# c spread from a row by TensorE, and the squares of x summed by TensorE ahead of the root's table

## The chip, the cores and the metric

The kernel runs on one core of one Trainium2 chip. The metric is device time in microseconds (us) of one execution; lower is better. Before the change three runs gave 1126.79 (median), 1125.45 and 1129.61 us.

## What is computed

A decoder trunk of two layers over 512 tokens of width 1024, in float32. Each layer is conditioned on a vector `c`: six vectors of width 1024 come from `silu(c) @ ada_w + ada_b`, and they scale, shift and gate the two halves of the layer. What the change touches is the very first step, the conditioned norm ahead of layer 0's projection:

```
def rms_norm(x, g):
    y = xf * lax.rsqrt(jnp.mean(xf * xf, axis=-1, keepdims=True) + EPS)
    return (y * g)
def adaln_params(c, w, b):
    m = jax.nn.silu(c) @ w + b
...
sh1, sc1, g1, sh2, sc2, g2 = adaln_params(c, ada_w[layer], ada_b[layer])
h = rms_norm(x, norm_mix_g[layer]) * (1.0 + sc1) + sh1
xr, gr, q, k, v = jnp.split(h @ ev_w_in[e], 5, axis=-1)
```

Then layer 0 runs a gated recurrence on `xr` (convolution, two gates by block matmuls, a scan), multiplied by `gelu(gr)`, beside a stick-breaking attention on `q`, `k`, `v`.

## The kernel before

x lies transposed in SBUF, channels on the 128 partitions in KC = 8 chunks of 128, tokens (512) along the free dimension. All large products are three matmuls of 512 columns (`mm3`): weights and activations are split into a rounded part and a rest (`whi`, `wlo`, and `hh`, `hl`), where ScalarE (ACT) writes the rounded part and VectorE (DVE) the rest. Weights come by DMA on SyncE's queue (SP) into `raw` tiles, three buffers in rotation; the gate pieces (`graw`, 128 KB) use the same three buffers.

The conditioning products are made on DVE: `ada_col` multiplies a 128x1024 block of `ada_w` with `c_s`, which holds silu(c) on every partition, and sums along the row. `c_s` is loaded by one DMA that repeats the row of c on 128 partitions (L119) and put through silu on ACT (L378).

The head of the kernel runs in this order. ACT: silu of `c_s`, then the table of Sqrt is called up by a dummy activation (`preload`, L326), then four squares of x (L394), two chunks each. DVE adds the two halves of each square (L395) and, in groups 1 and 2, the sum so far (L397); the sums of groups 2 and 3 go through TensorE (PE) against a column of `ones` (which holds 1/1024) into `ms` (L401, 4 calls of one column each). ACT takes the root (`sd`, L405), DVE the reciprocal (L408), PE spreads it over the partitions (`rb`, L412), DVE makes `ht` (L305), ACT `h` (L309), and the first projection product starts (L437). PE fills the time before with `busy(n)`: n products of `ones` with `ones` into a bank `warm` that nothing reads (L387). A call with float32 operands shows as two records in the trace.

These instructions are held in written order by `pin`. The first projection has eight accumulating banks (`qk`), fed chunk by chunk: for each m two conditioning columns, `ht`, the weight's rest and `hl` on DVE. Everything after it is put in order by a scheduler at build time, from its own estimates: an instruction's place on its engine is fixed before the run, and the engine then takes its instructions one after the other, waiting at each until its inputs are there. In layer 0's recurrence the pair of channel blocks (2, 3) follows the pair (0, 1); `pr` and `pi` are a block's gate products, `xcs` their input, `gw` the split gate piece, `gr` the products of the gelu branch. Three DMAs each of `k` and `kl` within SBUF, issued by POOL (L492), run beside it.

Of the kernel before, what the change touches and what calls it, by code (L numbers as in the profile page):

```python
# [9 lines left out]
F32 = mybir.dt.float32  # L10
F32R = mybir.dt.float32r
BF16 = mybir.dt.bfloat16
AF = mybir.ActivationFunctionType
ALU = mybir.AluOpType

P = 128
S = 512
D = 1024
KC = D // P
NB = S // P  # L20
# [47 lines left out]
def trunk(ctx, tc, xT, cvec, cols, adaw, wu, ws, w6, gate, cst, cstb, outT):  # L68
    nc = tc.nc
    V, A, PE = nc.vector, nc.scalar, nc.tensor  # L70

    const = ctx.enter_context(tc.tile_pool(name="const", bufs=1))
# [5 lines left out]
    def mm_bank(name):  # L78
        return pmm.tile([P, 512], F32, tag="mm", name=name)

    def aux_bank(name):
        return paux.tile([P, 512], F32, tag="aux", name=name)
# [7 lines left out]
    def pin(i):  # L90
        return tc.keep_in_program_order(i)


    c_s = const.tile([P, D], F32, name="c_s")
# [15 lines left out]
    ones = const.tile([P, P], F32, name="ones")  # L110
# [5 lines left out]
    dummy = const.tile([P, 1], F32, name="dummy")  # L116
    nsh = const.tile([P, KC], F32, name="nsh")

    nc.sync.dma_start(c_s, cvec.to_broadcast([P, D]))  # L119
    V.memset(ones, 1.0 / D)  # L120
    V.memset(zero, 0.0)
    V.memset(epst, EPS)
# [127 lines left out]
    def make_gs(l, ffn, m=0, w=KC):  # L250
        g = C(("nfg" if ffn else "nmg") + str(l), m, w)
        V.scalar_tensor_tensor(
            out=gs[:, 2 * l + ffn, m:m + w], in0=ada_ap(l, 4 if ffn else 1, m, w), scalar=1.0,
            in1=g, op0=ALU.add, op1=ALU.mult)
# [70 lines left out]
    def preload(func):  # L325
        pin(A.activation(dummy, epst, func))  # L326
# [35 lines left out]
    def first_col(s, m):  # L362
        return pin(ada_col(0, s, m, first[s, m]))
# [3 lines left out]
    def fetch_qk(m):  # L367
        load_first(1, m)
        load_first(0, m)
        qk_raw[m] = fetch(pending.pop(0))  # L370
# [4 lines left out]
        nc.sync.dma_start(x[:, m:m + 2], xT[:, m:m + 2])  # L375
    fetch_qk(0)
    fetch_qk(1)
    pin(A.activation(c_s, c_s, AF.Silu))  # L378
    preload(AF.Sqrt)
    nrm = Norm(0, 0)  # L380
    ms = aux_bank("ms0")
    warm = aux_bank("warm")

    def busy(n):

        for _ in range(n):
            pin(PE.matmul(warm[:, :P], ones, ones, start=True, stop=True))  # L387

    busy(34)
    with tc.high_priority():  # L390
        acc = None
        for m in range(0, KC, 2):
            s = wpool.tile([P, 2, S], F32, tag="whi", name=f"sq0_{m}")
            pin(A.activation(s, x[:, m:m + 2], AF.Square))  # L394
            pin(V.tensor_tensor(out=s[:, 0], in0=s[:, 0], in1=s[:, 1], op=ALU.add))  # L395
            if m in (2, 4):
                pin(V.tensor_tensor(out=s[:, 0], in0=s[:, 0], in1=acc, op=ALU.add))  # L397
            acc = s[:, 0]
            if m >= 4:
                for j in range(NB):  # L400
                    pin(PE.matmul(ms[:, j:j + 1], acc[:, j * P:(j + 1) * P], ones[:, 0:1], start=m + j == 4,  # L401
                                  stop=m + j == KC - 2 + NB - 1))
                busy(m // 2 - 2)
        sd = work.tile([P, NB], F32, tag="sd2", name="sd0")
        pin(A.activation(sd, ms[:, 0:NB], AF.Sqrt, bias=epst))  # L405
        first_col(1, 0)
        make_gs(0, 0, 0, 1)
        pin(V.reciprocal(sd, sd))  # L408
        first_col(0, 0)
        rb = aux_bank("rb0")  # L410
        for j in range(NB):
            pin(PE.matmul(rb[:, j * P:(j + 1) * P], sd[:, j:j + 1].to_broadcast([P, P]), ident, start=True, stop=True))  # L412
        busy(2)

        def first_weights():
            raw = qk_raw.pop(0)
            whi, wlo = (wpool.tile([P, 1024], F32R, tag=n, name=f"{n}_0") for n in ("whi", "wlo"))
            pin(V.tensor_copy(whi, raw))
            return whi, wlo, raw

        whi, wlo, raw = nrm.chunk(0, FULL, rb, pin, first_weights, lambda w:
                                  pin(V.tensor_tensor(out=w[1], in0=w[2], in1=w[0].bitcast(F32), op=ALU.subtract)))
        nrm.keep(rb, FULL, pin)
# [37 lines left out]
    for pair in ((0, 1), (4, 5), (2, 3), (6, 7)):  # L461
        s = {}
        for b in pair:
            c = b % 4
# [33 lines left out]
    for pair in ((0, 1), (2, 3)):  # L498
        r, ig, a, xc, bg, ge = {}, {}, {}, {}, {}, {}
        for c in pair:  # L500
# [5 lines left out]
            for s in (1, 2, 3):  # L506
                V.scalar_tensor_tensor(out=xc[c][:, s:], in0=bx[:, :S - s], scalar=C("cw", (3 - s) * 4 + c),
                                       in1=xc[c][:, s:], op0=ALU.mult, op1=ALU.add)
# [634 lines left out]
    s = [work.tile([P, S], F32, tag="sq", name=f"sqk1_{c}", bufs=2) for c in range(2)]  # L1143
# [279 lines left out]
```

## Time and profile before

| what | value |
|---|---|
| median of three runs | 1126.79 us |
| the profiled execution's own time | 1127.04 us |
| its span, first to last instruction | 1125.3 us |
| PE busy in the span | 1101.9 us (98%) |
| DVE busy | 810.0 us (72%) |
| ACT busy | 538.0 us (48%) |
| mean granted TensorE clock | 0.992 |
| first projection product | 18.15 us |
| largest idle time of PE | 7.25 us, ended at 121.78 us |

Times in the rows count from the first instruction. A row of the timeline gives start, duration, engine, line, operation, output and input tiles, how many instructions it merges, and in brackets the idle time before it with what ended it. PE is busy nearly all the time, so a saving elsewhere counts only where it ends one of PE's waits or lets PE start sooner; the granted clock says at which of its two levels (1.2 and 2.4 GHz) TensorE ran.

### The profile page before, as it was taken

The numbers are of one execution on the slowest core, as the hardware profiler recorded it, in microseconds if no ns is written. First come the engines' busy times: TensorE is split into PE (matmuls) and PEld (weight loads), VectorE is DVE, ScalarE is ACT, GpSimd is POOL, SyncE is SP. The second block draws the span as 40 slices with busy tenths as digits, with TensorE's granted clock in tenths as the row PEclk, the third lists the DMA queues.
The fourth block names the chain that finished last, engine by engine and source line by source line (L and its number), as shares of the span: only waits on it lengthen the run. The fifth ranks groups of instructions, "written<-read, shape, count | busy, mean of one in ns | idle before, by whom it ended". The sixth has DMA issues, their size and how long they took to land.

```text
span 1125.3 us, 16067 instructions
## 1 busy us (share of the span) xinstructions
PE 1101.9 (98%) x6212; PEld 930.7 (83%) x6212; DVE 810.0 (72%) x1262; ACT 538.0 (48%) x876; POOL 94.9 (8%) x91
## 2 busy tenths in 40 slices
PE   8999799999999999999999999999999999999998
PEld 7868576798888888888889876669999889998997
DVE  6966989877885378745657669987879449963773
ACT  4556778544332233312334566745566226641550
POOL 0001000000000000000000102210331033203200
PEclk8999899999999999999999999999999999999999
DMA  9849663524865257643432311121763656536612
GB/s 341 295 138 266 193 224 113 184 79 126 283 219 195 94 206 252 224 160 98 159 117 78 111 57 57 38 78 55 206 146 99 195 142 188 151 112 187 169 43 89
DMA packets 49146, 173.49 MB, mean 154 GB/s; under 512 B 5583, under 2 KB 6735, under 8 KB 48367
## 3 DMA queue, kind: packets, MB, share of 16 engines
q1 hardware_dynamic: 44542, 156.12, 41.4%
q0 software_dynamic: 4528, 16.35, 7.6%
q8 instruction: 49, 0.80, 0.3%
q14 instruction: 27, 0.22, 0.1%
HBM read 162.49 MB, written 2.10 MB: 146 GB/s over the span
## 4 chain that ended last, share of the span: by engine, by line
PE 87%; DVE 6%; ACT 3%; DMA 2%; issue 1%; DVEq 0%; ACTq 0%; SPq 0%
PE y L859 8%; PE d L209 7%; PE d L208 7%; PE d L207 7%; PE x L859 6%; PE g L208 4%; PE g L209 4%; PE u L209 4%; PE u L208 4%; PE g L207 4%; PE u L207 4%; PE o L207 3%; PE o L208 2%; PE o L209 2%; PE q L207 1%
## 5 line engine op out<-in xcount | busy, mean ns | idle before, releaser
L209 PE MATMUL d<-ah,wlo_d 128*128 128x512 f32 (+1 forms) x322 | 122.7, 381 | 0.0
L208 PE MATMUL d<-al,whi_d 128*128 128x512 f32 (+1 forms) x322 | 122.1, 379 | 0.0
L334 DVE SCALAR_TENSOR_TENSOR x<-d,ada,x 128x512 f32<-128x512 f32 (+1 forms) x51 | 36.7, 719 | 117.6 <-PE d L209 117.5
L207 PE MATMUL d<-ah,whi_d 128*128 128x512 f32 (+1 forms) x322 | 121.1, 376 | 0.0
L223 DVE CUSTOM_DVE_ANT_0 adaw<-adaw,c_s,col 128x1024 f32<-128x1024 f32 x80 | 99.6, 1278 | 4.8 <-DMA adaw<-adaw 4.6
L197 ACT ACTIVATE whi_d<-r_d 128x1024 fp32r<-128x1024 f32 (+1 forms) x40 | 40.8, 1019 | 111.8 <-PE d L208 74.7
L167 DVE TENSOR_TENSOR wlo<-raw,whi 128x1024 fp32r<-128x1024 f32 x49 | 59.7, 1220 | 19.7 <-ACT whi L166 18.8
L166 ACT ACTIVATE whi<-raw 128x1024 fp32r<-128x1024 f32 x49 | 51.8, 1057 | 41.4 <-PE o L208 22.1
L208 PEld LDWEIGHTS d<-al,whi_d 128*128 128x128 f32 x322 | 60.4, 188 | 12.6
L207 PEld LDWEIGHTS d<-ah,whi_d 128*128 128x128 f32 x322 | 60.5, 188 | 12.0
L209 PEld LDWEIGHTS d<-ah,wlo_d 128*128 128x128 f32 x322 | 60.5, 188 | 10.7
L209 PE MATMUL g<-h,wlo_g 128*128 128x512 f32 x176 | 69.4, 394 | 0.0
L209 PE MATMUL u<-h,wlo_u 128*128 128x512 f32 x176 | 69.4, 394 | 0.0
L208 PE MATMUL g<-h,whi_g 128*128 128x512 f32 x176 | 69.0, 392 | 0.0
L208 PE MATMUL u<-h,whi_u 128*128 128x512 f32 x176 | 69.0, 392 | 0.0
L207 PE MATMUL u<-h,whi_u 128*128 128x512 f32 x176 | 68.3, 388 | 0.0
L207 PE MATMUL g<-h,whi_g 128*128 128x512 f32 x176 | 68.3, 388 | 0.0
L197 ACT ACTIVATE whi_g<-r_g 128x1024 fp32r<-128x1024 f32 x22 | 23.4, 1062 | 68.6 <-PE g L208 50.9
L197 ACT ACTIVATE whi_s<-r_s 128x1024 fp32r<-128x1024 f32 x36 | 38.1, 1058 | 37.5 <-PE d L208 17.8
L787 POOL TENSOR_TENSOR r_s<-r_s,r_a 128x1024 f32<-128x1024 f32 x18 | 48.3, 2685 | 75.3 <-DVE gt L724 21.2
L198 DVE TENSOR_TENSOR wlo_s<-r_s,whi_s 128x1024 fp32r<-128x1024 f32 x36 | 48.4, 1343 | 8.6 <-ACT whi_s L197 7.9
L198 DVE TENSOR_TENSOR wlo_d<-r_d,whi_d 128x1024 fp32r<-128x1024 f32 (+1 forms) x40 | 46.8, 1170 | 9.9 <-ACT whi_d L197 7.9
(359 smaller groups left out, 3088.1 us busy)
## 6 DMA issues: line engine op xcount, KB each, us to landing
adaw<-adaw SPq DMA_DIRECT2D x80, 512.0 KB, 4.7
raw<-wu SPq DMA_DIRECT2D x56, 512.0 KB, 4.0
r_d<-wu SPq DMA_DIRECT2D x32, 512.0 KB, 3.6
r_a<-ws SPq DMA_DIRECT2D x27, 512.0 KB, 5.1
r_g<-wu SPq DMA_DIRECT2D x22, 512.0 KB, 3.5
r_u<-wu SPq DMA_DIRECT2D x22, 512.0 KB, 3.7
r_s<-ws SPq DMA_DIRECT2D x18, 512.0 KB, 4.7
r_s<-ws POOLq DMA_DIRECT2D x18, 512.0 KB, 6.2
```

Source lines behind the costliest of these rows:

```text
L166: pin(A.activation(hi, raw, AF.Copy))
L167: pin(V.tensor_tensor(out=lo, in0=raw, in1=hi.bitcast(F32), op=ALU.subtract))
L197: pin(A.activation(dst_hi, src, AF.Copy))
L198: pin(V.tensor_tensor(out=dst_lo, in0=src, in1=dst_hi.bitcast(F32), op=ALU.subtract))
L207: PE.matmul(out, whi, rhi, start=first, stop=False)
L208: PE.matmul(out, whi, rlo, start=False, stop=False)
L209: return PE.matmul(out, wlo, rhi, start=False, stop=last)
L223: return V.tensor_tensor_reduce(out=t, in0=t, in1=c_s, scale=1.0, scalar=C(f"ada_b{l}", s * 8 + m), op0=ALU.mult, op1=ALU.add, accum_out=a ...
L334: V.scalar_tensor_tensor(out=x[:, m, sl], in0=bank[:, sl], scalar=ada_ap(l, s, m), in1=x[:, m, sl], op0=ALU.mult, op1=ALU.add)
L787: G.tensor_tensor(out=self.t, in0=self.base[0].t, in1=self.base[1].t, op=ALU.add)
L859: m = [PE.matmul(out, w[a][:, o:o + P], b[c][:, k], start=slot in "AEF" and k + a + c == 0, stop=k == 3 and a == 1, skip_group_check=True) ...
```

## The change

c is loaded as one row of one partition (4 KB instead of 512 KB). Two products of K = 1, 512 columns each, spread it over the partitions: `ones[0:1]`, 1/1024 in each column, times half of the row; the silu reads them from PSUM with scale 1024, in two halves. They stand between 8 and 9 filler products, which were 34 in one row. The four squares of x follow the silu at once; the table of Sqrt is called up after them. DVE keeps four adds and loses the two that carried the sum on; PE sums all four groups (16 calls instead of 8), each followed by one filler. Three fillers instead of two follow `rb`.

```
-    nc.sync.dma_start(c_s, cvec.to_broadcast([P, D]))
+    c_row = const.tile([1, D], F32, name="c_row")
+    nc.sync.dma_start(c_row, cvec)
...
-    pin(A.activation(c_s, c_s, AF.Silu))
-    preload(AF.Sqrt)
...
-    busy(34)
+    busy(8)
+    for i in range(2):
+        cb = mm_bank(f"c{i}")
+        pin(PE.matmul(cb, ones[0:1], c_row[:, i * S:(i + 1) * S], start=True, stop=True))
+        pin(A.activation(c_s[:, i * S:(i + 1) * S], cb, AF.Silu, scale=float(D)))
+    busy(9)
...
-            if m in (2, 4):
-                pin(V.tensor_tensor(out=s[:, 0], in0=s[:, 0], in1=acc, op=ALU.add))
-            acc = s[:, 0]
-            if m >= 4:
-                for j in range(NB):
-                    pin(PE.matmul(ms[:, j:j + 1], acc[:, j * P:(j + 1) * P], ones[:, 0:1], start=m + j == 4,
-                                  stop=m + j == KC - 2 + NB - 1))
-                busy(m // 2 - 2)
+            for j in range(NB):
+                pin(PE.matmul(ms[:, j:j + 1], s[:, 0, j * P:(j + 1) * P], ones[:, 0:1], start=m + j == 0,
+                              stop=m + j == KC - 2 + NB - 1))
+            busy(1)
+        preload(AF.Sqrt)
...
-        busy(2)
+        busy(3)
```

Line numbers of the changed kernel are mostly one higher. ACT at the start, before:

```order
L378 ACT_TABLE_LOAD
L378 ACTIVATE c_s<-c_s 128x1024
L326 ACT_TABLE_LOAD
L326 ACTIVATE dummy<-epst 128x1
L394 ACTIVATE sq_0_164<-x 128x1024
L394 ACTIVATE sq_2_167<-x 128x1024
L394 ACTIVATE sq_4_171<-x 128x1024
L394 ACTIVATE sq_6_179<-x 128x1024
L405 ACTIVATE sd_187<-ms_128,epst 128x4
```

ACT at the start in the changed kernel, where `c_137` and `c_140` are the banks with the two halves of c:

```order
L393 ACT_TABLE_LOAD
L393 ACTIVATE c_s<-c_137 128x512
L393 ACTIVATE c_s<-c_140 128x512
L398 ACTIVATE sq_0_152<-x 128x1024
L398 ACTIVATE sq_2_160<-x 128x1024
L398 ACTIVATE sq_4_168<-x 128x1024
L398 ACTIVATE sq_6_176<-x 128x1024
L327 ACT_TABLE_LOAD
L327 ACTIVATE dummy<-epst 128x1
L406 ACTIVATE sd_185<-ms_127,epst 128x4
```

The table load and the dummy have moved from ahead of the squares to behind them.

PE at the start, before:

```order
L387 MATMUL warm<-ones 128x128 x34
L401 MATMUL ms_128<-ones,sq_4_171 128x1 x4
L401 MATMUL ms_128<-ones,sq_6_179 128x1 x4
L387 MATMUL warm<-ones 128x128
L412 MATMUL rb_193<-cs,sd_187 128x128 x4
L387 MATMUL warm<-ones 128x128 x2
```

PE at the start in the changed kernel:

```order
L386 MATMUL warm<-ones 128x128 x8
L392 MATMUL c_137<-c_row,ones 128x512
L392 MATMUL c_140<-c_row,ones 128x512
L386 MATMUL warm<-ones 128x128 x9
L401 MATMUL ms_127<-ones,sq_0_152 128x1 x4
L386 MATMUL warm<-ones 128x128
L401 MATMUL ms_127<-ones,sq_2_160 128x1 x4
L386 MATMUL warm<-ones 128x128
L401 MATMUL ms_127<-ones,sq_4_168 128x1 x4
L386 MATMUL warm<-ones 128x128
L401 MATMUL ms_127<-ones,sq_6_176 128x1 x4
L386 MATMUL warm<-ones 128x128
```

Four rounds of sums and filler stand now where two groups of sums stood, and the row of fillers is cut by the products of c.

The scheduler's order moves too, though the diff has no line there: on DVE, ACT, SP and PE between some 26 and 200 us of the trace of before; behind that the order is the same, and POOL's is the same throughout. In the recurrence, ACT around the tables of exp and gelu of the first pair, before (`a` and `r` are the recurrence's factors, `whi_884` a weight of the second pair's `gr`):

```order
L166 ACTIVATE whi_819<-raw_817 128x1024
L531 ACT_TABLE_LOAD
L531 ACTIVATE a_853<-r_754,s_84 128x512
L532 ACTIVATE r_754<-r_754,s_84 128x512
L531 ACTIVATE a_856<-r_774,s_84 128x512
L535 ACTIVATE a_859<-a_853 128x512
L532 ACTIVATE r_774<-r_774,s_84 128x512
L535 ACTIVATE a_862<-a_856 128x512
L166 ACTIVATE whi_884<-raw_882 128x1024
L539 ACT_TABLE_LOAD
```

The same place in the changed kernel (`gw_962` is the split gate piece of channel block 2, `graw_960` its load):

```order
L523 ACTIVATE r_773<-pr_765,col 128x512
L524 ACTIVATE ig_774<-pi_766,col 128x512
L532 ACT_TABLE_LOAD
L532 ACTIVATE a_852<-r_753,s_84 128x512
L198 ACTIVATE gw_962<-graw_960 128x256
L533 ACTIVATE r_753<-r_753,s_84 128x512
L532 ACTIVATE a_855<-r_773,s_84 128x512
L536 ACTIVATE a_858<-a_852 128x512
L533 ACTIVATE r_773<-r_773,s_84 128x512
L536 ACTIVATE a_861<-a_855 128x512
L540 ACT_TABLE_LOAD
```

The gate piece has come in between exp and tanh, and the weight `whi_884` has left; it stands behind the table of Sqrt now.

## Rows read from the trace of the kernel before

**Rows 1.** The page: span, and busy time of PE.

```profile
span 1125.3 us, 16067 instructions
PE 1101.9 (98%) x6212; PEld 930.7 (83%) x6212; DVE 810.0 (72%) x1262; ACT 538.0 (48%) x876; POOL 94.9 (8%) x91
```

**Rows 2.** Timeline of the head: start, duration, engine, line, tiles, count.

```profile
5.52 1.06 ACT L378 ACTIVATE c_s<-c_s 128x1024 f32<-128x1024 f32 x1 [3.49 <-DMA c_s<-cvec]
6.59 1.28 ACT L326 ACT_TABLE_LOAD   x1
...
8.00 4.08 ACT L394 ACTIVATE sq<-x 128x1024 f32<-128x1024 f32 x4
...
12.07 0.69 DVE L397 TENSOR_TENSOR sq<-sq,sq 128x512 f32<-128x512 f32 x1
12.68 0.69 DVE L395 TENSOR_TENSOR sq<-sq 128x512 f32<-128x512 f32 x1
...
12.91 1.92 PE L401 MATMUL ms<-ones,sq 128*128 128x1 f32 x16 [1.55 <-DVE sq L397]
...
15.39 1.16 PE L412 MATMUL rb<-cs,sd 128*128 128x128 f32 x8 [0.24 <-DVE sd L408]
...
16.59 0.75 DVE L305 SCALAR_TENSOR_TENSOR ht<-x,gs,rb 128x512 f32<-128x512 f32 x1
...
18.15 3.78 PE L437 MATMUL qk<-h,whi 128*128 128x512 f32 x8 [0.77 <-ACT h L309]
```

**Rows 3.** The loads of x: issues (first and last start), time to landing.

```profile
L375 SPq DMA_DIRECT2D x<-xT x4: 421/432/787, 1.2 to 2.6; - x4
...
DMA to landing us min/median/max: 5.6/7.2/8.4
```

**Rows 4.** Fillers on PE: busy time and records in two stretches of 4 us.

```profile
2.00:6.00 4.00, 4.00 (x21) 4.00 (x20) 1.00 0.92 236
7.00:11.00 4.00, 4.00 (x39) 4.00 (x38) 1.00 1.02 413
```

**Rows 5.** Timeline: ACT on 512 columns from PSUM; a float32 product of 512 columns.

```profile
18.00 0.58 ACT L297 ACTIVATE rstd<-rb 128x512 f32<-128x512 f32 x1
...
68.75 1.05 PE L126 MATMUL st<-sqk,cs 128*32 128x512 f32 x2
```

**Rows 6.** Stretches, all engines: PE, PEld, DVE, ACT, POOL busy; clock; DMA share; GB/s.

```profile
18.10:23.20 5.10, 5.05 (x12) 3.99 (x13) 5.07 (x9) 1.53 (x3) 0.00 (x0) 0.50 1.03 392
23.30:26.30 3.00, 3.00 (x14) 2.46 (x14) 3.00 (x7) 1.54 (x2) 0.00 (x0) 1.00 0.85 290
...
114.00:121.70 7.70, 0.53 (x3) 0.11 (x1) 7.70 (x12) 4.49 (x9) 0.00 (x0) 0.82 0.60 196
121.70:125.60 3.90, 3.82 (x9) 3.04 (x10) 3.90 (x7) 1.85 (x3) 0.00 (x0) 0.50 0.04 7
```

**Rows 7.** Chain that ended last, in order of time, from 84 to 123 us.

```profile
86.48 8.82 DMA raw<-wu
...
98.87 8.55 DMA adaw<-adaw
...
121.10 0.64 ACT xcs L197
...
121.78 0.80 PE pr L207
```

**Rows 8.** ACT's timeline in the same stretch.

```profile
103.46 1.04 ACT L166 ACTIVATE whi<-raw 128x1024 fp32r<-128x1024 f32 x1
...
109.49 1.26 ACT L539 ACTIVATE ge<-gr 128x512 f32<-128x512 f32 x2 [3.69 <-DVE r L536]
...
112.05 0.63 ACT L541 ACTIVATE r<-r 128x512 f32<-128x512 f32 x1
...
115.41 0.42 ACT L197 ACTIVATE gw<-graw 128x256 fp32r<-128x256 f32 x1 [0.81 <-DMA graw<-gate]
```

**Rows 9.** Loads of the gate pieces, 60 to 125 us: time to landing.

```profile
DMA to landing us min/median/max: 2.0/3.1/7.0
```

More of the change, by code (lines that the diff above doesn't have):

```diff
@@ L387, in busy @@
             pin(PE.matmul(warm[:, :P], ones, ones, start=True, stop=True))
-    busy(34)
+    busy(8)
[4 more added lines that the diff above has]
+    busy(9)
     with tc.high_priority():
-        acc = None
         for m in range(0, KC, 2):
```

## The prediction, made before the changed kernel ran

> **What bounds the kernel now.** I read the page first: PE is busy for 1101.9 of 1125.3 us [rows 1], so only PE's start and its few waits have anything to give. Then I read the timeline of the head, where the edit lies. The reader is to see one string: silu of c ends at 6.58, the table of Sqrt takes 1.28 us, the squares run from 8.00 to 12.08, DVE's last add from 12.68 to 13.37, PE's sums to 14.83, `rb` to 16.55, `ht` from 16.59, the first projection product at 18.15 [rows 2]. Last I read the stretches with the granted clock, since two places run at half rate: after the head, and after PE's largest wait [rows 6]. That wait, 114 to 121.7, is not in the diff, but the scheduler's new order goes through it, so its chain and ACT's rows there are read too [rows 7 to 9].
>
> **The head, step by step.** c as a row. PE reaches c's first product after 8 fillers. Cold, 20 weight loads fall in 4 us, warm 38 [rows 4], so a record costs about 0.2 or 0.105 us, and 16 cold records end near 1.06 + 3.4 = 4.45. The row must have landed by then. No load of 4 KB is in the trace; the nearest is the gate piece of 128 KB, 2.0 us at best [rows 9], the other end is the wait that the repeated load caused, silu starting at 5.52 [rows 2] after an issue at 0.74, 4.8 us. Landing lies between 2.7 and 5.5; I take 3, being far smaller, so the fillers hide it.
>
> The products of c. Each has two records of 512 columns, four times a filler's: 1.7 us cold, 0.85 warm; the float32 product of 512 columns in the trace takes 1.05 from start to end [rows 5]. K = 1 is not in the trace; I price it as K = 128, with nothing below. The fillers of before turn warm between 6 and 7 us [rows 4]. So the first half ends near 6.2, the second near 7.2, and the second silu (512 columns from PSUM, 0.58 [rows 5]) at 7.8. Were both cold: 8.5.
>
> The squares. They start at 7.8 instead of 8.00: the 1.28 us of the table have left the path, but c comes 1.2 us later. The last x landed at 2.6 + 8.4 = 11.0 [rows 3], which is when the last square of before could begin. With 508 KB less ahead of x, at the 413 GB/s of [rows 4], it lands 1.2 us earlier, 9.8, before it is wanted (7.8 + 3 x 0.95 = 10.65). The squares end at 11.7.
>
> The adds and sums. DVE no longer carries the sum on; two adds of 0.69 go [rows 2]. The last add ends at 11.7 + 0.7 = 12.4, against 13.37. But PE now has four groups: 16 records in 1.92 us were two groups [rows 2], so 0.95 a group, and 0.2 for its filler, 1.15, more than the 0.95 at which squares come. Starting at 9.65, when the first add is done, the fourth ends at 9.65 + 4 x 1.15 - 0.2 = 14.05, plus some 0.1 to drain: 14.15 against 14.83. So of 1.0 us on DVE, 0.7 is left on PE. The table of Sqrt behind the squares is done at 11.7 + 1.28 + 0.2 = 13.2, hidden under the sums with 0.9 to spare. In the trace a table load begins 0.01 after the activation before it and costs 1.28. The Trainium skill (ScalarE: Activation LUTs, What ACT_TABLE_LOAD costs) counts about 2.66 us with a drain; by that the root would wait until about 14.6 and only 0.25 of the gain would be left. From `rb` on nothing changes but time: the projection starts at 17.45 instead of 18.15, **-0.7**. Bounds: if the clock falls before `rb` (the sums keep the array less busy than 34 fillers did), its 8 records cost 1.6 instead of 1.16 and the sums some more, and the gain is 0.
>
> What is left of it. The first 24 products run at clock 0.50 until about 23.2, 12 of them in 5.1 us [rows 6]. If the clock comes back when it did, 0.7 us more at half rate is worth 0.35. **Step: -0.35.** Ends: 0, and -2.9 if the clock never falls there (5.1 us at half rate are 2.55 more). DVE, busy 5.07 of the 5.10 us, would cap that near -2.4.
>
> **The moved order.** Before, PE waits from 114.3 to 121.78 for `xcs` of block 2. Its chain runs through loads that wait their turn beside the copies of `k` and `kl`: a weight (8.82 us to land), a conditioning block (8.55, landing at 107.42), behind which DVE holds back the product that gelu waits for [rows 7, 8]. The new order moves the split of the weight of `xr2` on ACT and DVE ahead of the `kn` products. That delays `k`, its copies and the first `xcs` by some 1.5 to 2 us, covered by ten `gr` products that now stand ahead of `pr` on PE (10 x 0.23). In return SP can issue the next weight near 78 instead of 86.48, so one block fewer stands in the crowd, and the gate piece of block 2 lands near 105 instead of 107.6 (100.6 + 7.0 [rows 9]; the loads behind one another landed some 2 to 4 us apart). But ACT now meets that gate piece between exp and tanh, and waits. Queued behind it: tanh, exp, two squares, tanh (3.0 us, before done while DVE waited), the table of gelu (1.28), two gelu (1.26), the table of Sqrt (1.28), the root. So the root starts at 105 + 0.4 + 3.0 + 1.28 + 1.26 + 1.28 = 112.2 against 112.05 [rows 8]: the gain of the load is used up. Behind the root stands the weight split that ran at 103.46 before, 1.06. It frees the buffer for the second gate piece, whose load is then issued near 115.8 instead of 111.2. With the copies gone it lands in 2 us, at 118, against 115.4 [rows 8]. ACT meets it ahead of the second root and the second `xc`. This shifts the second `xc` chain on DVE by some 2 us: **PE's wait ends +1.7 later.** In it three more `gr` products fit (17 instead of 14 ahead of `pr`), 3 x 0.23 = **-0.7** behind it. Bounds of the +1.7: -3 if the gate piece lands at 100, +4 if it lands at 107.6 like before.
>
> **Sum** against the profiled execution, 1127.04: -0.35 + 1.7 - 0.7 = +0.65, 1127.7. The median of before lies 0.25 under that execution. Forecast **1127.5**, no change by what a measurement can tell here (about 0.5%, 5.6 us).
>
> **The rivals.**
> A. The clock stays up or comes back sooner in the head, because sums and fillers follow each other without a gap from 9.65 on. For it: before, PE stood idle for 1.55 us ahead of the sums [rows 2] and the clock was at 0.50 when the projection began [rows 6]. Against: a filler of 0.2 in each 1.15 us is little work for the array, since a sum has one column. Time: -2.4 in place of -0.35, 1125.5. The Trainium skill (TensorE: Matmul & The Clock Gate, Why this matters for your kernels) gives this rule, that a busy TensorE keeps its full clock; the half rate after PE's wait [rows 6] agrees, no row shows it for sums of one column.
> B. The crowd of loads clears sooner and PE's wait shrinks. For it: one weight leaves the crowd. Against: the loads are in one queue and the copies are as many as before. Gate piece at 100 to 102: -3 to -1.5 in place of +1.7; less idle time may save the half rate behind it (3.9 us at 0.50, [rows 6]), another -1.9. Time: 1121 to 1124, the middle 1122.5.
> C. Slower: ACT, held by the gate piece, holds back everything behind it. It decides if that piece lands at 107.6 or later: then the root is 2.5 later, the second gate piece too, PE's wait ends +4 and the clock, lost for longer, comes back one stretch later (another +1.9): +5.2 with the head's gain, 1132.
> D. The change doesn't do what it says: the row of c lands at 5.5 or both products run cold, so the squares start at 8.5 and the sums, bound by PE, end no earlier than before. Head 0 to +0.5: 1128.2.
>
> **How the numbers follow.** Forecast 0.50, A 0.18, B 0.16, C 0.10, D 0.06. The range 1123.0 to 1131.5 takes in the forecast's own ends, A, D, the upper two thirds of B and most of C: about 0.85. Faster by over 0.5% needs 1121.2: the lower part of B, or B with A, 0.10. Slower by over 0.5% needs 1132.4: half of C and what else the new order may do between 130 and 200 us, 0.08. The rest, 0.82, is within 0.5%.
>
> **What would show it.** Right: first square near 7.8, last add near 12.4, the first projection product near 17.5 at clock 0.50, the table of Sqrt ending before the sums; ACT idle for some 3 to 5 us ahead of the first split of a gate piece of the second pair; `pr` of block 2 near 123. Wrong: a first product at clock 1.00 (A), that split without a wait (B) or `pr` past 125 (C), a silu of c after 8 us (D). I would be wrong as a whole if the trace differed from before by more than 2 us behind 200 us, where the order is the same.

## The result, and the profile of the changed kernel

The changed kernel takes 1133.47 us (median of 22 runs, 1128.88 to 1137.24) against 1127.59 us of the kernel before (22 runs beside it, 1123.18 to 1132.96): a ratio of 1.0058, 95% interval 1.0045 to 1.0072. It is slower by 5.9 us where no change was forecast, and lies 2 us above the range. The profiled execution is the slowest of the 22, 1137.24 us. Two executions of later kernels that took far longer, 1826.63 us in experiment 4 and 2208.56 us in experiment 9, stand in no ratio below.

The page of the changed kernel, against [rows 1]: PE is busy 10 us longer with six records fewer, so its loss is one of rate more than of waits.

```profile
span 1135.5 us, 16050 instructions
PE 1112.2 (98%) x6206; PEld 939.2 (83%) x6206; DVE 810.0 (71%) x1260; ACT 537.9 (47%) x877; POOL 94.7 (8%) x91
```

The timeline of the head, against [rows 2] (start, duration, engine, line, tiles, count; in brackets the idle time before and what ended it):

```profile
4.55 1.98 PE L392 MATMUL c<-c_row,ones 1*128 1x512 f32 x4
...
6.57 0.60 ACT L393 ACTIVATE c_s<-c 128x512 f32<-128x512 f32 x1 [0.26 <-PE c L392]
...
7.06 3.88 ACT L398 ACTIVATE sq<-x 128x1024 f32<-128x1024 f32 x4
...
9.39 1.71 PE L401 MATMUL ms<-ones,sq 128*128 128x1 f32 x8
...
10.96 1.28 ACT L327 ACT_TABLE_LOAD   x1
10.98 0.69 DVE L399 TENSOR_TENSOR sq<-sq 128x512 f32<-128x512 f32 x1 [0.25 <-ACT sq L398]
...
11.52 1.71 PE L401 MATMUL ms<-ones,sq 128*128 128x1 f32 x8
...
15.79 1.71 PE L401 MATMUL ms<-ones,sq 128*128 128x1 f32 x8
...
17.53 0.27 ACT L406 ACTIVATE sd<-ms,epst 128x4 f32<-128x4 f32 x1 [5.07 <-PE ms L401]
...
18.06 2.07 PE L413 MATMUL rb<-cs,sd 128*128 128x128 f32 x8
...
21.73 2.12 PE L438 MATMUL qk<-h,whi 128*128 128x512 f32 x8 [0.31 <-ACT h L310]
```

c, the squares and DVE's adds come early: the last add ends at 11.67, against 13.37. PE's sums are what comes late. A group with its filler takes 11.52 - 9.39 = 2.13 us, the root waits 5.07 us for them, and the first projection product starts at 21.73 instead of 18.15. The stretches of PE with the granted clock say why (stretch, length, PE busy and records, clock, DMA share, GB/s):

```profile
4.30:7.60 3.30, 3.30 (x17) 1.00 1.02 414
7.70:21.30 13.60, 13.60 (x64) 0.50 0.79 302
21.40:26.40 5.00, 4.69 (x21) 1.00 0.77 273
```

The clock falls to 1.2 GHz near 7.7, just behind the products of c, and stays there until the projection begins, although PE has no idle time in these 13.60 us. Before, it was at 1.00 through fillers and sums (7.7 to 14.7 us) and at 0.50 from 18.1 on [rows 6].

The middle, ACT's timeline and then PE's, against [rows 8] and [rows 7]:

```profile
108.13 0.42 ACT L198 ACTIVATE gw<-graw 128x256 fp32r<-128x256 f32 x1 [5.53 <-DMA graw<-gate]
...
115.13 0.63 ACT L542 ACTIVATE r<-r 128x512 f32<-128x512 f32 x1
...
118.23 0.40 ACT L198 ACTIVATE gw<-graw 128x256 fp32r<-128x256 f32 x1
```

```profile
125.67 0.79 PE L208 MATMUL pr<-xcs,gw 128*128 128x512 f32 x1 [8.09 <-ACT xcs L198]
```

ACT is held for 5.53 us by the gate piece of block 2 and everything behind it is late: the root by 3.1 us, `pr` of block 2 by 3.9, of which 1.9 came in with PE (the end of `xr`). Why the gate piece is late shows in the chain of work that ended last, each step released by the one before it (start, duration, what):

```profile
88.86 9.40 DMA raw<-wu
...
99.43 1.24 DVE wlo L168
100.69 7.42 DMA graw<-gate
```

Its load is issued when DVE is done with a weight in the ring (99.43 + 1.24 = 100.67 us), and takes 7.42 us to land.

The last rows are PE's waits between 150 and 240 us, the first line from the kernel before, the second from the changed one (engine, line, waited for: us in total, times, longest):

```profile
PE z L587 <- DVE q L198: 1.0, 1, 1.0
```

```profile
PE z L588 <- DVE q L199: 1.9, 2, 1.5
```

So the 5.4 us by which PE is late at 241 us were lost at three places. They can be read from the starts of four products on PE's timeline: the end of `qk` (the first projection), the first `v`, the first `z` (attention) and the first `g` (feed-forward). The lines of `g`, before and changed:

```profile
240.89 0.39 PE L207 MATMUL g<-h,whi 128*128 128x256 f32 x1 [1.43 <-ACT h L309]
```

```profile
246.31 0.38 PE L208 MATMUL g<-h,whi 128*128 128x256 f32 x1 [1.43 <-ACT h L310]
```

| | end of `qk` | to the first `v` | first `z` to first `g` | first `g` |
|---|---|---|---|---|
| before | 64.36 | 69.90 | 84.17 | 240.89 |
| changed | 65.91 | 71.97 | 86.03 | 246.31 |
| lost | 1.55 | 2.07 | 1.86 | 5.42 |

Behind `g` the delay stays within 5.4 to 5.6 us up to 860 us. From there this one execution loses another 4.7, mostly by products that run 4% slower. The kernel before has such products too; how often each kernel meets them is not known (last section).

### The profile page after: what moved, and what is told of

It reads as the page before. It is cut to its first block, busy times and chain, and to the rows that moved or that the text cites. A ratio compares the mean times of both kernels' runs of the same rounds, so it can differ in the third digit from the quotient of the medians.

```text
span 1135.5 us, 16050 instructions
## 1 busy us (share of the span) xinstructions
PE 1112.2 (98%) x6206; PEld 939.2 (83%) x6206; DVE 810.0 (71%) x1260; ACT 537.9 (47%) x877; POOL 94.7 (8%) x91
## 4 chain that ended last, share of the span: by engine, by line
PE 88%; DVE 5%; ACT 4%; DMA 2%; issue 1%; DVEq 0%; ACTq 0%
PE y L860 9%; PE d L210 7%; PE d L209 7%; PE d L208 7%; PE x L860 7%; PE g L209 4%; PE g L210 4%; PE u L210 4%; PE u L209 4%; PE g L208 4%; PE u L208 4%; PE o L208 2%; PE o L210 2%; PE o L209 2%; PE q L208 1%; PE ov L1223 1%
## 5 line engine op out<-in xcount | busy, mean ns | idle before, releaser
L168 DVE TENSOR_TENSOR wlo<-raw,whi 128x1024 fp32r<-128x1024 f32 x49 | 59.7, 1220 | 18.4 <-ACT whi L167 17.6
```

What stands on the lines that cost most here:

```text
L168: pin(V.tensor_tensor(out=lo, in0=raw, in1=hi.bitcast(F32), op=ALU.subtract))
```

## The experiments

**Theories.** 1: the products of c over one partition row lose the clock, and the head costs the time. 2: the four thin groups of sums with one filler each lose it. 3: the scheduler's moved order between 26 and 200 us costs the time, whatever the head does. A fact helps to tell them apart: the order behind the head is settled at build time, and small edits of the head flip it. So a kernel can have the old head with the new order, or the new head with an order like the old one. The second column names the order by the kernel that has it; the third order and those with the gate early belong to neither kernel of the case. The times up to `g` are read from one trace of each kernel. All ratios are to the kernel before, run on the same chip.

| kernel | order behind 26 us | end of `qk` | `qk` to `v` | `z` to `g` | first `g` | ratio, 95% interval |
|---|---|---|---|---|---|---|
| before, second profile | before's | 64.30 | 69.73 | 84.17 | 240.67 | 0.9990, 0.9968 to 1.0013 |
| changed | changed | 65.91 | 71.97 | 86.03 | 246.31 | 1.0058, 1.0045 to 1.0072 |
| 1 row of c, old sums | third | 64.24 | 68.12 | 83.80 | 238.61 | 1.0025, 1.0006 to 1.0044 |
| 2 c broadcast, new sums | changed | 63.94 | 71.98 | 87.22 | 245.53 | 1.0063, 1.0039 to 1.0087 |
| 3 c over 128 rows | third | 64.73 | 68.29 | 83.80 | 239.28 | 1.0019, 1.0002 to 1.0036 |
| 4 three fillers | changed | 69.70 | 72.32 | 85.86 | 250.28 | 1.0061, 1.0038 to 1.0084 |
| 5 table late only | changed | 61.93 | 71.83 | 85.82 | 241.97 | 1.0052, 1.0035 to 1.0069 |
| 6 changed, 16 fillers | near before's | 66.32 | 70.28 | 84.18 | 243.22 | 1.0034, 1.0013 to 1.0055 |
| 7 before, 28 fillers | third | 66.82 | 69.12 | 83.80 | 242.15 | 1.0008, 0.9989 to 1.0026 |
| 9 as 5, gate early | gate early | 62.90 | 68.13 | 83.78 | 237.21 | 0.9974, 0.9960 to 0.9988 |
| 10 before, gate early | gate early, 2 | 64.27 | 66.54 | 83.80 | 237.22 | 0.9981, 0.9963 to 0.9998 |
| 11 before, 8 fillers behind | third | 65.40 | 69.60 | 83.78 | 241.18 | 1.0036, 1.0021 to 1.0050 |
| 12 as 10 and 11 | gate early, 3 | 66.20 | 67.36 | 83.78 | 239.75 | 0.9996, 0.9980 to 1.0011 |
| 13 changed, gate early | as 9 | 65.87 | 68.21 | 83.79 | 240.26 | 1.0000, 0.9981 to 1.0020 |
| 14 as 13, 128 rows | PE as 9 | 64.31 | 68.32 | 83.79 | 238.82 | 0.9993, 0.9976 to 1.0009 |

**1. Row of c, sums as before.** In the changed kernel:

```
-            for j in range(NB):
-                pin(PE.matmul(ms[:, j:j + 1], s[:, 0, ...], ones[:, 0:1], start=m + j == 0, ...))
-            busy(1)
+            if m in (2, 4): ... acc ...      # adds and two groups as before
```

> The c row is spread by its four products as in the changed kernel and the root's table comes after the squares, but the sums of squares are taken as before (adds carried by VectorE, two sum groups at its end). The middle of the program has the order of the kernel before. Theory 1 (the products of c over one partition row are what loses the clock): the granted clock falls to 0.50 near 8 us as in the changed kernel, the sums run at 1.7 us a group, and the first projection product comes at about 19.5 us instead of 18.15. Theory 2 (the four thin sum groups with one filler each are what loses it): the clock stays at 1.00 until about 16 us and the first projection product comes at 17.5 to 18.2. Theory 3 (the moved order behind 26 us costs the most): time within 1.5 us of the kernel before whatever the head does, since the order here is that of before; theory 1 or 2 alone, with the middle blameless, would leave +1 to +3 and 0 in turn.

Measured: 0.50 from 7.6 to 21.2, first projection product at 19.71. Theory 1 called both. Theory 2 is against it: these sums are the old ones. The order behind 26 us is not that of before, as was expected, but a third one. The time, +0.25%, is less than half of the changed kernel's loss, but more than the 1.5 us that theory 3 allowed; and since `g` starts 2.3 us earlier than before on the trace, the trace up to there does not explain it.

**2. c by broadcast, new sums.** In the changed kernel the broadcast load, one silu and `busy(34)` are put back; sums and table stay.

> c comes by the broadcast load with one silu and 34 fillers as before, the four sum groups with one filler each and the late table as in the changed kernel; the middle has exactly the order of the changed kernel. Theory 1: without the products of c the clock is at 1.00 until about 16 us, a sum group with its filler takes 1.15 us, and the first projection product comes at 17.0 to 17.6. Theory 2: the clock falls within the sum groups, between 10 and 14 us, and the first projection product comes at 19 to 21 us. Theory 3: whatever the head does, block 2's pr is about 4 us later than before (ScalarE held some 5 us by the gate's piece near 103 us) and the whole is 3 to 5 us over the kernel before; if the head alone were to blame, the whole would be within 1 us of the kernel before under theory 1.

The timeline of PE, and the stretch with its clock:

```profile
10.54 0.95 PE L396 MATMUL ms<-ones,sq 128*128 128x1 f32 x8
...
11.66 0.95 PE L396 MATMUL ms<-ones,sq 128*128 128x1 f32 x8
...
15.41 2.08 PE L408 MATMUL rb<-cs,sd 128*128 128x128 f32 x8 [0.24 <-DVE sd L404]
```

```profile
4.90:15.00 10.10, 10.10 (x92) 1.00 1.02 403
```

The same four thin groups run at full clock, 11.66 - 10.54 = 1.12 us a round. So theory 2 falls, and the forecast's price of a round was right for this clock. The first projection product came at 19.08, not at 17.0 to 17.6, as the sums began only at 10.54, the clock fell when they were done and `rb` ran at half rate. And with `qk` ending 0.4 us earlier than before the kernel is as slow as the changed one: theory 3.

**3. c over 128 rows.**

```
-    c_row = const.tile([1, D], F32, name="c_row")
-    nc.sync.dma_start(c_row, cvec)
+    c_row = const.tile([P, D], F32, name="c_row")
+    V.memset(c_row, 0.0)
+    nc.sync.dma_start(c_row[0:1], cvec)
...
-        pin(PE.matmul(cb, ones[0:1], c_row[:, i * S:(i + 1) * S], start=True, stop=True))
+        pin(PE.matmul(cb, ones, c_row[:, i * S:(i + 1) * S], start=True, stop=True))
```

> The changed kernel with the products of c over all 128 partition rows (the row loaded into the first row of a zeroed tile), so that the same columns are streamed with the whole array's rows in use; the middle falls into the order of the kernel before. Theory 1: the clock stays at 1.00 past 8 us, the sum rounds take 1.15 us instead of 2.13, the first projection product is at about 17.5 us and the whole is within 1 us of the kernel before. Theory 2: the clock falls near 8 to 12 us all the same, the first projection product is at 20 to 22 us. Theory 3: within 1.5 us of the kernel before even if the head is late, as the order is that of before.

```profile
8.10:14.80 6.70, 6.35 (x53) 1.00 1.02 400
```

With the same columns over all rows the clock stands behind the products of c. The first projection product came at 20.22 all the same, since here the clock rose only at 8.1 and the two products, from 5.70 to 8.75, ran mostly at half rate: the 17.5 was a miss. So was the order, which is the third and not that of before, and the time: +0.19% is 2 us, where 1 or 1.5 were allowed, though `g` starts 1.6 us earlier than before.

**4. Three fillers behind each group.** `busy(1)` in the loop of sums becomes `busy(3)`.

> The changed kernel with three fillers behind each sum group instead of one; its order in the middle is that of the changed kernel. Theory 2 (too few fillers between the groups): the clock is at 1.00 through the sums, a round takes 0.85 + 0.65 = 1.5 us, the first projection product is at 17.5 to 18.5 us. Theory 1: the clock still falls near 7.7 us, before the first sum group, and the fillers only lengthen the rounds, from 2.13 to about 3.0 us: the first projection product at about 24 to 25 us and the whole 1 to 3 us over the changed kernel. Theory 3: whole 3 to 5 us over the kernel before in either case.

```profile
7.50:24.50 17.00, 17.00 (x81) 0.50 0.69 263
```

Theory 1 again: the fillers only lengthen the rounds, and the first projection product comes at 24.85. The whole is no slower than the changed kernel within the intervals, though the first `g` is 4 us later. On the two traces that comes back behind 860 us: the slower products of the last section fill nearly all of that stretch in the changed kernel's trace and none of it in this one, and a wait of PE for weights, 1.15 us near 867, is gone too. Whether the medians come together for the same reason is not shown.

**5. The table moved, nothing else.**

```
-    preload(AF.Sqrt)
     nrm = Norm(0, 0)
...
+        preload(AF.Sqrt)
         sd = work.tile([P, NB], F32, tag="sd2", name="sd0")
```

> The kernel before with one line moved: the load of the root's table stands behind the squares. Nothing else of the change is in it, yet its order behind 26 us is that of the changed kernel, instruction for instruction but for four on VectorE. Theory 3 (the moved order costs the time): the first projection product stays within 0.5 us of 18.15, ScalarE waits 5 us or more for block 2's gate piece near 100 us, PE's wait before pr is about 8.1 us instead of 7.25, v starts 1.5 to 2.5 us late, another 1 to 2 us go between 160 and 200 us, and the time is 1131 to 1133 us against 1127. Theory 1 or 2 (the head costs it): within 1 us of the kernel before, since its head is almost untouched.

PE's and ACT's timelines:

```profile
17.77 2.11 PE L437 MATMUL qk<-h,whi 128*128 128x512 f32 x8 [1.15 <-ACT h L309]
```

```profile
104.33 0.42 ACT L197 ACTIVATE gw<-graw 128x256 fp32r<-128x256 f32 x1 [5.61 <-DMA graw<-gate]
...
111.33 0.63 ACT L541 ACTIVATE r<-r 128x512 f32<-128x512 f32 x1
```

This run weighs most. The head starts its first product 0.38 us earlier than before, no product over one row is in it, and the time is 1133.01 us, +0.52%: with the moved order and a head nearly untouched, the loss is like the changed kernel's. Its marks are there: the hold of 5.61 us, 71.83 us from `qk` to `v`, 85.82 from `z` to `g`. From the end of `qk` to the first `g` it takes 180.0 us, the changed kernel 180.4, the kernel before 176.5. That `v` would be late was a miss. In this execution the clock did not fall in the head at all (1.00 from 6.6 to 115.7), `qk` ended 2.4 us early, and the order gave that back and 1.1 us more by the first `g`. The rest of this execution's +4.9 us come behind 860 us, with the slower products there (last section). So the median's loss is not placed by this one trace in full.

**6. The changed kernel with 16 fillers ahead of c.** `busy(8)` becomes `busy(16)`.

> The changed kernel with 16 instead of 8 fillers ahead of the products of c; all else of the change is in it (row of c, four sum groups, late table), but its order behind 26 us is close to that of the kernel before: the gate's piece stands where it stood. Theory 3: 0 to 3 us over the kernel before (1127 to 1130), although the first projection product is 2 to 4 us late. Theory 1 or 2: 5 to 6 us over it, as the changed kernel, since its head is as late as that one's.

PE's timeline and stretches:

```profile
7.15 1.98 PE L392 MATMUL c<-c_row,ones 1*128 1x512 f32 x4
9.06 3.90 PE L386 MATMUL warm<-ones 128*128 128x128 f32 x18
12.80 0.39 PE L401 MATMUL ms<-ones,sq 128*128 128x1 f32 x3
```

```profile
6.00:9.30 3.30, 3.30 (x17) 1.00 0.99 348
9.40:12.70 3.30, 3.30 (x18) 0.50 1.03 422
12.80:16.20 3.40, 3.40 (x33) 1.00 1.02 419
```

Here PE is already at full clock when the products of c begin, and the clock falls as they are done. It is back at 12.8, after nine fillers in a row, and the thin groups behind run at full clock. The whole change with nearly the old order costs 0.34%: less than the changed kernel's 0.58%, though the two intervals overlap, and more than nothing. So the head has its own part, some 2 us at the end of `qk`, and 0.4 us more up to `g`.

**7 and 11. The third order with the old head.** In experiment 7 `busy(34)` becomes `busy(28)`; in 11 the loop's `busy(m // 2 - 2)` becomes `busy(8 if m == 6 else 0)`.

> The kernel before with 28 instead of 34 fillers ahead of the sums, which gives it, behind 26 us, the very order of the first and third experiment. If what those two gained between 64 and 240 us (2.2 and 1.6 us more than the kernel before at 240 us, with later heads) is the order's: first projection product at 18 to 19 us, v 1.5 to 3 us earlier than before, and 1124 to 1126 us. If the gain was only where the granted clock happened to be lost in those two executions: within 1.5 us of the kernel before, with v as late as before.

> The kernel before with eight fillers instead of one behind the second sum group, which gives it the order of the first, third and seventh experiment behind 26 us, with all of its 34 fillers ahead of the sums kept. The head: rb about 1.1 us later, first projection product at 19.0 to 19.5 us; with the array busier around the root the clock may stay at 1.00. If that order is 1.2 to 2.2 us better between 64 and 240 us, as those three profiles read: v 1 to 3 us earlier than before and 1124.5 to 1126.5 us. If it is only different: 1127 to 1129.

In both, `g` follows `qk` sooner than before (175.3 and 175.8 us against 176.5), so the third order is a little better; but both heads end `qk` later, by 2.5 us (the clock falls at 12.2, while PE stands idle for 3.17 us ahead of the sums) and by 1.0 us. Neither kernel gains, and both forecasts of an earlier `v` and a shorter time were misses; that the eleventh is 0.36% slower while its `g` starts only 0.3 us late is not explained by its trace up to there.

**8. The kernel before, again.**

> The kernel before, unchanged, for a second profile. If the middle repeats: the first product at 18.15 and v at 134.3 within 0.5 us. If the stretches at half clock near 119 to 126 and 180 to 184 us fall differently in another execution: v and the products at 240 us up to 3 us earlier or later, which then is no effect of an edit. The last 200 us have y and x products of 0.1133 us in the first profile; a cadence of 0.1178 as in the changed kernel's profile would add about 5 us and be the spread of the runs.

PE's products repeat to 0.35 us up to 820 us. So differences of 2 us between traces up to there come from the edits, or from where the clock was lost, as far as one repetition can tell.

**9 and 10. The gate pieces loaded early**, in the kernel of experiment 5 and, as a control, in the kernel before:

```
     for pair in ((0, 1), (2, 3)):
         r, ig, a, xc, bg, ge = {}, {}, {}, {}, {}, {}
+        gr_ = {}
+        for c in pair:
+            gr_[c] = work.tile([P, 256], F32, tag="graw", name=f"graw{c}", bufs=2)
+            nc.sync.dma_start(gr_[c], gate[c])
...
-            graw = raw_tile(f"graw{c}")
-            nc.sync.dma_start(graw[:, :256], gate[c])
+            graw = gr_[c]
```

> The fifth experiment (the kernel before with only the root's table moved, in the changed kernel's order) with the gate's two pieces of a pair in tiles of their own, loaded at the head of the pair, so that ScalarE cannot be held by them near 100 us. If the hold of ScalarE is most of what the moved order costs: no wait for the gate's piece, the root of block 0 some 4 us earlier than there, PE's wait before pr under 6.5 us instead of 8.1, v 1.5 to 3 us earlier than in the fifth experiment, and 1128.5 to 1131 us against 1133. If VectorE's waits for the conditioning blocks or the chain after 160 us are the cost: v no earlier, time within 1.5 us of the fifth experiment's 1133.

> The same edit (gate pieces in tiles of their own, loaded at the head of the pair) on the kernel before, whose ScalarE waits only 0.8 us for a gate piece: the control. If the hold is what the edit cures, there is little to cure here: within 1.5 us of the kernel before, 1126 to 1129. If loading the gate early is good for something else too (the crowd of loads between 87 and 108 us): 1123 to 1126.

ACT's timeline and PE's wait (64 to 140 us) in experiment 9:

```profile
94.44 0.42 ACT L197 ACTIVATE gw<-graw 128x256 fp32r<-128x256 f32 x1 [5.29 <-DMA graw<-gate]
```

```profile
PE pr L207 <- ACT xcs L197: 5.0, 2, 4.2
```

Taken literally the expectation was wrong: ACT is still held, for 5.29 us. But the hold has moved from 104 to 94 us, ahead of block 1's `xcs` and no longer between exp and tanh. PE waits 4.2 us there, and for block 2 only 0.8 instead of 8.1. The time falls from +0.52% to -0.26%, further than forecast, while on the old order the same edit is worth 0.19%. Both kernels are faster than the two of the case. Both have their first `g` at 237.2, but in experiment 9 `qk` had ended 1.37 us earlier: from there to `g` it takes 174.3 us against 172.9. With the gate pieces in the weights' ring of three buffers it was 180.0 (experiment 5) against 176.5. So the moved order costs 3.5 us with the pieces in the ring and 1.4 us with them early; 2.1 us of it go with the edit, and 3.6 us are gained on the old order as well. The edit moved PE's order too, so it shows the place of the loss, not each step of it.

**12. Gate early and eight fillers together**, on the kernel before.

> The edits of the two last kernels together on the kernel before: gate pieces loaded at the head of the pair, and eight fillers behind the second sum group. If both gain, 1121 to 1125 us, under both kernels of the case; if the gate's early load gains nothing, as the eleventh experiment, 1124.5 to 1128.

Its head ends `qk` 1.8 us late, and the two edits together come out as the kernel before. The best of the study stay experiments 10 and 9, 1124.68 and 1125.02 us.

**13 and 14. The changed kernel with the gate early.** The edit of experiment 9, and `c_row` in a tile of the weights' ring, because the row's own tile leaves too little room; in 14 the products of c over 128 rows as in experiment 3.

> The changed kernel, whole, with the gate's pieces in tiles of their own and loaded at the head of the pair, and the row of c in a tile of the weights' ring to make room; its order behind 26 us is that of the ninth experiment but for four instructions of VectorE. If the loss of the changed kernel is the hold's alone: 0.0 to 0.4% under the kernel before, as the ninth (1123.5 to 1127.5). If the head costs by itself, with its clock lost near 7.7 us and the first projection product near 21.7 us: qk's end 1.5 to 2.5 us later than before and 0.1 to 0.4% more than the ninth experiment, 1126 to 1130.

> The kernel of the thirteenth experiment with the products of c over all 128 rows of a zeroed tile; PE's order is the same. If the clock lost behind the products over one row is what the head costs: clock at 1.00 to about 15 us, first projection product 1 to 1.5 us earlier than in the thirteenth (the products themselves are 1.1 us longer at half clock), and a time 0 to 1.5 us under it. If it costs nothing behind qk's end: the same time within 1 us.

Against the changed kernel, experiment 13 has the same head (`qk` ends at 65.87 and 65.91) and takes back as much as it lost: 6.05 us at the first `g`, 0.58% in time. Part of this is a gain that the same edit has on the old order too (experiment 10). Against experiment 9 it has the same order and the changed head, and costs 2.97 us at the end of `qk`, 3.05 at the first `g`, 0.26% in time; the two intervals just overlap. Over 128 rows the first projection product and the end of `qk` come 1.56 us earlier, just above the 1 to 1.5 expected for the product, and the times differ by 0.07%, which these runs can't tell apart. PE's timeline and the stretch behind the rise of the clock in experiment 14:

```profile
5.71 2.35 PE L393 MATMUL c<-c_row,ones 128*128 128x512 f32 x4
```

```profile
6.70:13.40 6.70, 6.35 (x49) 1.00 1.02 402
```

Here the clock was up for most of the products, and it stayed up behind them, though not to 15 us as expected.

## Why the prediction was wrong, step by step

The forecast was +0.65 us on the trace; it was 5.42 at the first `g`.

**What held.** The row of c landed under the fillers: its first product started at 4.55, forecast 4.45. The two products took 1.98 us, less than the 2.75 forecast (4.45 to 7.2), and the second silu ended at 7.2 instead of 7.8; squares and adds followed 0.7 us early. The table of Sqrt ended at 12.24 and the dummy behind it began at 12.26, after which ACT waited 5.07 us for PE. The longer price of the Trainium skill (ScalarE: Activation LUTs, What ACT_TABLE_LOAD costs) was not seen. A round of sums and filler at full clock is 1.12 us (experiment 2), forecast 1.15.

**The step that failed first is the pricing of the products of c "as K = 128, with nothing below".** Their duration was right, but not what they do to the clock. In all five executions with products over one row (the changed kernel and experiments 1, 4, 6, 13) the granted clock fell to 0.50 within 1.3 us of their end; in none of the eleven others did it fall before 12 us. When it had risen does not tell them apart: at 4.1 to 6.0 us in the five, at 3.9 to 8.1 in the others. So the round took 2.13 us, `rb` 2.07, and the first product came 3.58 us late, where the prediction's worst bound for that case was a gain of 0. It saw a fall of the clock only between the sums and `rb`. Since the clock then rose as the projection began, 2.0 us came back; the step, forecast -0.35, measured +1.55.

The Trainium skill (TensorE: Matmul & The Clock Gate, Why this matters for your kernels) gives the rule that a TensorE kept busy keeps its full clock. The changed kernel's 13.60 us at 0.50 without idle time, filled with fillers, one-column sums and `rb`, do not agree with it, and the measurement decides. Rival A, built on that rule, is out for the changed kernel; in experiment 5 its picture (a head that keeps its clock, `qk` 2.4 us early) did occur, to the amount forecast, without such products.

**The second is the middle, +1.7 - 0.7 = +1.0 forecast, 2.07 measured.** The hold was the one described: ACT meets the gate piece between exp and tanh and waits, for 5.53 us where some 3 to 5 were named. The three `gr` products did give 0.7 back: PE's last `pr` is 4.31 us late, its first `v` 3.62. What was mis-sized is the landing of the gate piece. Counted from the end of `qk` it landed 42.2 us on instead of 43.3, 1.1 us sooner, where 2.6 were forecast; the load was issued at 100.69, as late as before, and still took 7.42 us. With the head's delay on top it landed at 108.11, and the root started at 115.13 instead of 112.2. And the +1.7 hung on the wrong load: the forecast had the root on time and the second gate piece late, issued near 115.8 and landing at 118. It was issued at 109.76 and landed at 117.08, and ACT, itself late, took it at 118.23 without a wait. What makes `pr` late is the root, by 3.1 of its 3.9 us.

**That is rival C, and it was given 0.10.** Its condition, a gate piece at 107.6 or later, held (108.11); it named +4 for the end of PE's wait (3.9), `pr` past 125 (125.67), a clock lost for longer behind it (120.3 to 130.6 us, instead of 118.9 to 125.7), and 1132 us. Its price was met by two parts that the prediction kept apart: half of `pr`'s delay came from the head. The forecast's terms were summed as if the head's gain could only help the middle; a head that is late by 1.5 us brings the forecast's own mechanism to C's condition.

**The third was not in the sum at all.** Between the first `z` and the first `g` the changed order loses 1.86 us; the three other kernels with that order (experiments 2, 4, 5) lose 1.65 to 3.05 there, and no kernel with another order loses anything. The prediction named "what else the new order may do between 130 and 200 us" in a chance, without a price. PE waits there for DVE (`z` for `q`, 1.9 us instead of 1.0; all its waits there come to 3.2 us instead of 1.8), and the conditioning blocks stand at other places of DVE's order; which of these moves is the cause was not tried.

**How the whole loss divides.** Up to `g` the traces divide it. From the end of `qk` to `g` the four kernels with the changed order (changed, 2, 4, 5) take 180.0 to 181.6 us, those with the order of before or one near it (before twice, 6) 176.4 to 176.9. The medians point the same way: the four are 0.52 to 0.63% slower whatever their head, the three with most of the changed head and another order (1, 3, 6) 0.19 to 0.34%. So the order carries most of the loss. Of its 3.5 us, 2.1 go when the gate pieces leave the weights' ring, and 1.4 stay (5 and 9 against before and 10). The head with the order held costs 0.26% (13 against 9), 2 to 3 us.

What stays open is how the medians come out of the traces. The order's 0.52% and the head's 0.26% do not add up to 0.58%, and the medians of experiments 1, 3, 5 and 11 lie some 3.5 to 5 us higher than their first `g` tells. The slower products of the last section could be the reason, but with one trace of each kernel, and two of before, no run shows how often an execution meets them. The clock alone is not the reason: over the 22 runs of the changed kernel the mean granted clock goes from 0.988, that of the profiled execution, to 0.995, and the five runs at 0.994 or more (median 1135.82 us) were no faster than the five at 0.988 (1132.85 us).

The range and the chances failed because the scheduler's moves were priced as one small term, and 0.82 was put on "no change". The prediction's own sign of being wrong as a whole, over 2 us of difference behind 200 us, was met with 5.42. From the end of `qk` to the first `g`, the orders compared here lie between 2.2 us less and 5.1 us more than before's 176.5, with the gate pieces in the ring.

Three details of the prediction do not hold, without weight in its sum: rows 6 show 12 products by 23.2 us, not 24; PE's wait began at 121.78 - 7.25 = 114.53, not 114.3; and rival C's +5.2 is 4 + 1.9 - 0.7, which with the head's -0.35 would be +4.85, 1131.6 us.

## What to carry to other kernels

When a small edit passes through a scheduler, compare the order first and price the moved order as its own change; an edit that keeps the old order (here, eight more fillers) is a cheap test of which of the two costs. A load that shares a rotating buffer with the weights is taken when the ring has room, not when it is needed: small pieces that an in-order engine will meet deserve buffers of their own. Products that use one row of the array fill its time but did not hold its clock here; spread over all rows, the same columns did.

## What the runs showed of the hardware that was not expected

The fall of the clock behind products over one partition row is told above. Behind it, at 0.50, the clock did not rise in 13.6 and 17.0 us in which PE ran rounds of one-column sums with one filler or three (the changed kernel, experiment 4). It rose after nine fillers in a row (experiment 6, 9.06 to 12.96 us). The same nine stand behind the products of c in the changed kernel, but only 1.7 us of them lay behind the fall, and it did not rise there. At 1.00 the same rounds ran without a fall (experiment 2).

The products of 256 columns in the last 200 us have two speeds at granted clock 1.00. Rows of the groups by line, 1045 to 1090 us, of the kernel before and of the changed one (busy us, mean ns):

```profile
L859 PE MATMUL x<-h,whi_a 128*128 128x256 f32 x32 | 5.5, 276 | 0.0
```

```profile
L860 PE MATMUL x<-h,whi_a 128*128 128x256 f32 x32 | 5.7, 280 | 0.0
```

From start to start it is 0.113 or 0.118 us, some 4%. Against the kernel before, the stretch behind 860 us is 3.7 to 4.7 us longer in the traces of the changed kernel and of experiments 5, 11 and 14, nearly all at the slower spacing; in those of experiments 4, 6, 7 and 13 no product there has it. No edit is needed for it: in the second profile of the kernel before one line has both (count, minimum, median, maximum in ns, 930 to 970 us).

```profile
L859 PE MATMUL y<-h,whi_a x69: 276/276/280, 930.7 to 969.9; 128*128 128x256 f32 x69
```

It could make up much of the 10 us over which the runs of one kernel spread, and it makes up most of the 4.7 us by which the changed kernel's profiled execution is later than its 5.5 at 820 us. What switches it, and whether it comes equally often in every kernel, no run shows.
